# Sample states, convolution rows and vectors in the chip's order, and the samples' state step on turned states

## The chip, the cores and the metric

The kernel runs on one core of a Trainium2 chip. It is one launch. The metric is the device time of that launch in microseconds (us). The engines named below are those of the profile: PE is TensorE's matrix multiply and PEld its weight load, DVE is VectorE, ACT is ScalarE, POOL is GpSimd, and SP is SyncE, whose queue issues nearly all transfers (DMAs) of this kernel. Each engine takes its instructions strictly in the order in which they were written into its stream, and an instruction that waits for a semaphore holds up all that stand behind it.

## The reference, cut to what matters

One step of a decoder with two layers: first a Mamba-2 state-space layer (SSD), then latent attention (MLA). A prompt of 1024 tokens and 8 samples of 8 tokens each go through both. Only the SSD layer, and in it mostly the samples' part, is touched here.

```python
def causal_conv(xbc, buf, w, b):              # xbc: 4096 columns; buf: the last 3 rows of each sample
    full = jnp.concatenate([buf, xbc], axis=1)
    out = full[:, 0:t] * w[0]
    for k in range(1, 4):
        out = out + full[:, k:k + t] * w[k]
    return out + b, full[:, full.shape[1] - 3:]          # the second result is returned: new state_conv

def ssd_scan(x, dt, a_head, bm, cm, init_state):         # 32 heads of 64, 8 groups of 4 heads, state width 128
    ...
    def step(s, inp):                                    # s: (heads, 64, 128) for each sample or the prompt
        st, dec = inp
        return dec[..., None, None] * s + st, s
    final, prev = lax.scan(step, init_state, (states, chunk_decay))
    y_off = jnp.einsum('bclgn,bcgrpn->bclgrp', cc, prev) * decay_in[..., None]
    y = (y_diag + y_off).reshape(b, L, h, p)
    return y, final                                      # final is returned: new state_ssm
```

For a sample the scan has one step: the new state of each head is a decay times the old state (64 by 128, `state_ssm`), plus an outer product summed over the 8 tokens of B (128 wide) with the weighted inputs x (64 wide). The samples' output `y` takes C (128 wide) times the old state.

## The kernel before, in words

All products run on PE in float32 halves: a value is split into a high part (a cast on ACT) and a low part (value minus high part, on DVE or POOL; `split`, lines 125 to 133), and three products replace one.

The SSD layer has 8 groups of 4 heads. A group has a projection part (`Group`): four blocks of 128 columns (B, C and two of x), each made in three pieces of 24 matmuls into the PSUM tile `pj` (line 86; two such tiles take turns), copied to `raw` by ACT (lines 508 to 511), then convolved with 1 step on ACT (line 521) and 3 on DVE (line 525), then Silu on ACT (line 481). `gates` makes nine more pieces `pz` (line 98) that ACT copies to `z` and puts through Silu in three instructions (lines 569, 571, 572).

Then the group is scanned. `ssd_chunks` goes through the eight chunks of the prompt and the samples' tokens as a ninth: it reads a block `M` of cumulative decays by a DMA (line 627; three such tiles take turns), adds a mask on DVE (628), takes Exp on ACT in four instructions (632), multiplies on DVE (633), and multiplies with x on PE (`py`, 637). `ssd_states` does the samples' states in four parts per group (two halves of the samples, `q`, by two pairs of heads, `pr`): a state tile `s0` is loaded (711), turned on PE by four transposes into the PSUM tile `s0p` (714), split into `sh` and `sl`, multiplied with C (`pv`, 723); POOL multiplies the loaded tile with the decay (727), PE makes the outer product `sn` (730) from x and a copy `bb` of B that POOL spread over four samples (705), DVE adds it (732), and the tile is stored (733). The state tile lies with head and head-row on the partitions and the state width along them, as in the reference; the product with C needs it the other way round.

The projection of group g+1 and the scan of group g are written in turns (`layer_ssd`), and a scheduler that plans with its own table of times then sets the order in which the instructions stand in each engine's stream. So a change to a few instructions can move others. The tables that Exp and Silu need on ACT are not the same, and an `ACT_TABLE_LOAD` stands wherever the two follow each other.

Vectors (norm weights, convolution weights) are loaded as rows and turned on PE (lines 199 to 209); the samples' convolution rows are loaded as 96 rows and turned by eight transposes (`conv_state_T`, 356 to 362); the new rows of a group, collected in `ct` by POOL (518, 519), are turned by four transposes into `ctp` (533), copied to `co` by DVE (535), which takes a `raw` tile for it, and stored by six DMAs (538, 539). The prompt's last state is turned by two transposes (`pf`, 666), copied (668) and stored (669).

## Time and profile before

| what | us |
|---|---|
| median of 3 runs (1922.32 to 1925.89) | 1924.01 |
| the profiled execution's own time | 1926.24 |
| its span | 1924.4 |
| PE busy | 1890.9 (98%) |
| DVE busy | 1206.0 (63%) |
| ACT busy | 1102.0 (57%) |
| POOL busy | 823.3 (43%) |

The profile is of one execution, 2.23 us above the median. The span is the time from its first to its last instruction, and 1.84 us lie around it. PE's busy time counts matmuls that overlap, so that it does not say how fast PE works; what one matmul costs is read from the chain that ended last, which counts it from its start to the next one's. The SSD layer takes about the first half of the span: norm and the first group's projection until about 119 us, eight scans until about 890 us, and the output product until about 1010 us. The rest is MLA.

### The profile page before, as it was taken

The page shows a single profiled execution, that of the slowest core. Times are in us where ns is not written, and L with a number is a line of the kernel's source. Part 1 is how long each engine was busy: PE and PEld are TensorE (multiplying, and loading weights), DVE is VectorE, ACT ScalarE, POOL GpSimd, SP SyncE. Part 2 cuts the span into 40 slices and gives each one's busy share as a digit, 9 for nine tenths or more (in the row PEclk, how much of TensorE's full clock was granted, in tenths as well). Part 3 has the DMA queues.
Part 4 walks back from the last instruction along what each step waited for, and adds up shares of the span by engine and source line. Part 5 has one row for each costly group of instructions (what it writes and reads, how often), then busy time and mean ns, then how long its engine had stood idle before and what let it go on. Part 6 is the DMA issues. An engine that isn't in the chain of part 4 may idle for free.

```text
span 1924.4 us, 33639 instructions
## 1 busy us (share of the span) xinstructions
PE 1890.9 (98%) x12023; PEld 1728.8 (90%) x12023; DVE 1206.0 (63%) x2500; ACT 1102.0 (57%) x2523; POOL 823.3 (43%) x1122
## 2 busy tenths in 40 slices
PE   8999999999999999999999999999999999899998
PEld 7999999999999999888788998998888888788887
DVE  5557676757676757665534114567877888766674
ACT  6467566667666666733214314436777777755552
POOL 2447555545654555443004222104433435774551
PEclk9999999999999999999999999999999999999999
DMA  5223323333333232645534343123111112754541
GB/s 165 53 78 91 96 79 98 86 104 86 97 83 98 85 98 81 212 152 175 164 109 129 114 163 87 63 102 96 49 47 41 52 41 60 207 185 150 156 129 39
DMA packets 181087, 202.02 MB, mean 105 GB/s; under 512 B 18828, under 2 KB 147608, under 8 KB 180536
## 3 DMA queue, kind: packets, MB, share of 16 engines
q1 hardware_dynamic: 175864, 180.08, 30.9%
q0 software_dynamic: 4976, 19.66, 3.2%
q8 instruction: 95, 1.56, 0.4%
q14 instruction: 72, 0.59, 0.1%
q10 hardware_dynamic: 80, 0.13, 0.0%
HBM read 146.52 MB, written 53.28 MB: 104 GB/s over the span
## 4 chain that ended last, share of the span: by engine, by line
PE 84%; ACT 4%; DVE 4%; DMA 4%; issue 2%; POOL 1%; SPq 0%; POOLq 0%; DVEq 0%; ACTq 0%
PE pj L86 22%; PE pz L98 7%; PE pq L98 6%; PE pob L98 5%; PE p L98 5%; PE poa L98 3%; PE py L637 2%; PE sc L86 2%; PE o L86 2%; PE sc L1376 2%; PE o L1439 2%; PE o L1441 2%; PE st L1408 2%; PE st L1409 2%; PE st L1410 2%
## 5 line engine op out<-in xcount | busy, mean ns | idle before, releaser
L86 PE MATMUL pj<-xl,wih 128*128 128x384 f32 (+1 forms) x768 | 255.4, 333 | 0.0
L86 PE MATMUL pj<-xh,wih 128*128 128x384 f32 (+1 forms) x768 | 252.9, 333 | 1.2 <-ACT xh L273 0.9
L86 PE MATMUL pj<-xh,wil 128*128 128x384 f32 (+1 forms) x768 | 252.9, 329 | 0.0
L1422 POOL TENSOR_TENSOR tl<-P,th 128x384 fp32r<-128x384 f32 (+1 forms) x96 | 90.5, 942 | 234.3 <-ACT P L1420 192.7
L525 DVE SCALAR_TENSOR_TENSOR acc<-raw,vec,acc 128x1112 f32<-128x1112 f32 x96 | 140.9, 1469 | 14.9 <-ACT acc L521 14.0
L86 PEld LDWEIGHTS pj<-xh,wih 128*128 128x128 f32 x768 | 143.8, 188 | 2.6 <-ACT xh L273 1.4
L86 PEld LDWEIGHTS pj<-xl,wih 128*128 128x128 f32 x768 | 144.5, 188 | 1.0
L86 PEld LDWEIGHTS pj<-xh,wil 128*128 128x128 f32 x768 | 144.5, 188 | 0.5
L98 PE MATMUL pz<-wih,xh 128*128 128x256 f32 x504 | 143.2, 288 | 1.2 <-ACT z L566 1.2
L98 PE MATMUL pz<-wil,xh 128*128 128x256 f32 (+1 forms) x504 | 139.7, 283 | 0.0
L1419 ACT ACTIVATE th<-st 128x512 fp32r<-128x512 f32 x192 | 94.8, 494 | 66.7 <-PE st L1415 51.0
L98 PE MATMUL pz<-wih,xl 128*128 128x256 f32 x448 | 128.5, 287 | 0.0
L632 ACT ACTIVATE M<-M,tok 128x128 f32<-128x128 f32 (+1 forms) x288 | 90.8, 388 | 58.5 <-DVE M L628 58.1
L1712 POOL TENSOR_TENSOR kvl<-pgr,kvh 128x256 fp32r<-128x256 f32 x128 | 97.3, 787 | 57.0 <-ACT kvh L1710 52.6
L133 DVE TENSOR_TENSOR wil<-wraw,wih 128x512 fp32r<-128x512 f32 x88 | 73.9, 845 | 39.6 <-ACT wih L127 33.6
L98 PEld LDWEIGHTS pz<-wih,xh 128*128 128x128 f32 x504 | 95.9, 190 | 2.2 <-ACT z L566 1.7
L1420 ACT ACTIVATE P<-st 128x512 f32<-128x512 f32 x192 | 93.8, 489 | 0.0
L98 PEld LDWEIGHTS pz<-wil,xh 128*128 128x128 f32 (+1 forms) x504 | 92.8, 184 | 0.1
L1422 DVE TENSOR_TENSOR tl<-P,th 128x512 fp32r<-128x512 f32 x96 | 74.3, 774 | 19.6 <-ACT P L1420 19.5
L98 PEld LDWEIGHTS pz<-wih,xl 128*128 128x128 f32 x448 | 85.3, 190 | 0.7
L613 POOL TENSOR_TENSOR xdd<-xsT,tok 128x256 f32<-128x256 f32 x64 | 48.7, 761 | 86.8 <-ACT xsT L599 83.9
L127 ACT CAST wih<-wraw 128x512 fp32r<-128x512 f32 x92 | 56.1, 618 | 44.9 <-PE pj L86 29.4
(833 smaller groups left out, 6274.6 us busy)
## 6 DMA issues: line engine op xcount, KB each, us to landing
wraw<-in_ssd_w_in SPq DMA_DIRECT2D x92, 256.0 KB
M<-acs_d SPq DMA_DIRECT2D x64, 256.0 KB
s<-in_state_ssm SPq DMA_DIRECT2D x32, 256.0 KB
y_d<-y SPq DMA_DIRECT2D x64, 128.0 KB
out_s_ssm<-s SPq DMA_DIRECT2D x32, 256.0 KB
q_d<-qt SPq DMA_DIRECT2D x32, 192.0 KB
qp<-q_d SPq DMA_DIRECT2D x8, 768.0 KB
wraw<-in_ssd_w_out SPq DMA_DIRECT2D x10, 512.0 KB
```

Of the source, the lines that this page charges most:

```text
L86: nc.tensor.matmul(out, a, b, start=(i == 0), stop=(i == n - 1))
L98: nc.tensor.matmul(o, a, b, start=(j == 0), stop=(j == len(ops) - 1))
L127: k.cast = nc.scalar.copy(hi, src)
L133: return (eng or nc.vector).tensor_tensor(lo, src, hi.bitcast(F32), op=ALU.subtract)
L525: last = nc.vector.scalar_tensor_tensor(acc, raw[:, j : j + n], k.convw[j][:, blk : blk + 1], acc, op0=ALU.mult, op1=ALU.add)
L613: nc.gpsimd.tensor_tensor(v3(xdd), v3(xsT), hb(2), op=ALU.mult)
L632: nc.scalar.activation(M[:m, h, :m], M[:m, h, :m], AF.Exp, bias=tk[:, 0, 4 * g + h : 4 * g + h + 1])
L637: nc.tensor.matmul(py[:m, h * 64 : h * 64 + 64], M[:m, h, :m], xsT[:m, h * 64 : h * 64 + 64], start=True, stop=True)
L1419: nc.scalar.activation(th[:, :n], ps[:, :n], AF.Exp, scale=SCALE)
L1420: nc.scalar.activation(P[:, :n], ps[:, :n], AF.Exp, scale=SCALE)
L1422: eng.tensor_tensor(tl[:, :n], P[:, :n], th[:, :n].bitcast(F32), op=ALU.subtract)
L1712: nc.gpsimd.tensor_tensor(rl[:, j], raw[:, j], rh[:, j].bitcast(F32), op=ALU.subtract)
```

## The change

numpy lays out four inputs before the launch and puts three outputs into the reference's order after it. In the kernel:

- The vectors come as one tile of 128 by 196 by one DMA; the five loads, two transposes and a copy go.
- The samples' convolution rows come in the order of `convT` by one DMA; four loads, eight transposes and two copies go.
- The new convolution rows are stored as they lie in `ct`, by one DMA per group; four transposes, a copy and five DMAs per group go.
- The prompt's last state is stored as it lies; two transposes and a copy per group go.
- The samples' states come with the state width on the partitions. The four transposes per part go, and `split` reads the loaded tile in SBUF. The decay is multiplied along the other axis (its small table `decs` is made by one matmul with ones and has 256 columns instead of 128), and the outer product is made the other way round: B is now the operand that is loaded, and x is spread over the samples by POOL, once for each pair of heads (`xb`, two per half instead of one `bb`).

```diff
-def load_vectors(k, vp, psum):
+def load_vectors(k):
     nc, I, cp = k.nc, k.I, k.cp
     nc.sync.dma_start(k.ident, I["c_ident"])
-        r1 = vp.tile([128, 128], F32, name="r1")
-        nc.sync.dma_start(r1, I["ssd_conv_w"].rearrange("o k (b c) -> (o k b) c", c=128))
...
-        nc.tensor.transpose(p[:, :128], r1, k.ident)
-        nc.tensor.transpose(p[:, 128:196], r2, k.ident[:68, :68])
-        nc.vector.tensor_copy(k.vec, p[:, :196])
+    k.vec = cp.tile([128, 196], F32, name="vec")
+    nc.sync.dma_start(k.vec, I["vec"])
...
             def after():
-                conv_state_T(k, p0, psum)
+                k.nc.sync.dma_start(k.convT, k.I["state_conv"])
...
     def conv_out(self):
-        for bi in range(4):
-            nc.tensor.transpose(p[:27, bi * 128 : bi * 128 + 128], self.ct[:, bi], k.ident)
-        co = self.rp.tile([128, RAW], F32, tag="raw", name=f"co{g}", bufs=2)[:27, :512]
-        nc.vector.tensor_copy(co, p[:27])
-        sc = k.O["s_conv"].rearrange("o b w c -> (o b w) c")
-        for o, n, c in ((0, 128, DIN + 128 * g), (128, 128, DIN + 1024 + 128 * g), (256, 256, 256 * g)):
-            nc.sync.dma_start(k.O["p_conv"][0, 0, :, c : c + n], co[0:3, o : o + n])
-            nc.sync.dma_start(sc[:, c : c + n], co[3:27, o : o + n])
+        k, g = self.k, self.g
+        k.nc.sync.dma_start(k.O["conv"][g], self.ct)
...
         if i == 7:
-            for pr in range(2):
-                nc.tensor.transpose(pf[:, pr * 128 : pr * 128 + 128], S[:, pr * 128 : pr * 128 + 128], k.ident)
-            fo = sp.tile([128, 256], F32, tag="fo", name="fo" + tag, bufs=1).rearrange("p (a n) -> p a n", a=2)
-            nc.scalar.copy(fo, pf[:, :256].rearrange("p (a n) -> p a n", a=2))
-            nc.sync.dma_start(k.O["p_ssm"][0, 0, 4 * g : 4 * g + 4].rearrange("(a h) p n -> (h p) a n", h=2), fo)
+            nc.sync.dma_start(k.O["p_ssm"][g], S)
...
-        bb = sp.tile([96, 4, 128], F32R, tag="bb", name=f"bb{tag}{q}", bufs=1)
-        nc.gpsimd.tensor_tensor(bb, b3.bitcast(F32).unsqueeze(1).to_broadcast([96, 4, 128]),
-                                k.blk3.unsqueeze(2).to_broadcast([96, 4, 128]), op=ALU.mult)
         for pr in range(2):
             s0 = sp.tile([128, 4, 128], F32, tag="s0", name=f"s0{tag}{q}{pr}", bufs=2)
-            nc.sync.dma_start(s0, I["state_ssm"][0, bs, h0 : h0 + 2].rearrange("b h p n -> (h p) b n"))
-            for b in range(4):
-                nc.tensor.transpose(pt[:, b * 128 : b * 128 + 128], s0[:, b], k.ident)
+            nc.sync.dma_start(s0, I["state_ssm"][pair][:, bs])
+            xb = sp.tile([96, 4, 128], F32R, tag="bb", name=f"xb{tag}{q}{pr}", bufs=1)
+            nc.gpsimd.tensor_tensor(xb, x3[:, 128 * pr : 128 * pr + 128].bitcast(F32).unsqueeze(1).to_broadcast([96, 4, 128]),
+                                    k.blk3.unsqueeze(2).to_broadcast([96, 4, 128]), op=ALU.mult)
...
-            split(k, sh, sl_, pt)
+            split(k, sh, sl_, s0.rearrange("p b n -> p (b n)"))
...
-            nc.gpsimd.tensor_tensor(s0, s0, k.decs[:, h0 // 2, bs].unsqueeze(2).to_broadcast([128, 4, 128]),
+            nc.gpsimd.tensor_tensor(sv, sv, k.decs[:, bs, h0 : h0 + 2].unsqueeze(3).to_broadcast([128, 4, 2, 64]),
                                     op=ALU.mult)
-            nc.tensor.matmul(pt, x3[:, pr * 128 : pr * 128 + 128], bb.rearrange("p b n -> p (b n)"),
-                             start=True, stop=True)
+            nc.tensor.matmul(pt, b3, xb.rearrange("p b n -> p (b n)"), start=True, stop=True)
...
-            nc.sync.dma_start(k.O["s_ssm"][0, bs, h0 : h0 + 2].rearrange("b h p n -> (h p) b n"), s0)
+            nc.sync.dma_start(k.O["s_ssm"][pair][:, bs], s0)
```

The scheduler writes another order. Line numbers of the changed kernel are smaller, by 11 at the norm and by 39 to 46 in the scan. First PE, at the first samples' part of the scan of group 2. Before, the four transposes stand in the first chunk's products:

```order
L86 MATMUL st_0_3798<-xddh_0_3777,BTh_0_3771 128x256
L86 MATMUL pj<-xh,wih 128x384
L714 MATMUL s0p_800_3875<-ident,s_800_3873 128x128 x4
L86 MATMUL st_0_3798<-xddl_0_3778,BTh_0_3771 128x256
L86 MATMUL st_0_3798<-xddh_0_3777,BTl_0_3772 128x256
L637 MATMUL py_0_3793<-xsT_0_3769,M_0_3785 128x64 x4
```

Now the product with C (`pv`, line 677) stands there, since it needs nothing of PE ahead of it:

```order
L598 MATMUL py_0_3684<-xsT_0_3660,M_0_3676 128x64 x4
L86 MATMUL st_0_3689<-xddh_0_3668,BTh_0_3662 128x256
L677 MATMUL pv_800_3770<-sh_800_3766,cblk_1091 64x128
L677 MATMUL pv_800_3770<-sl_800_3767,cblk_1091 32x128 x2
L677 MATMUL pv_800_3770<-sh_800_3766,cblk_1091 64x128
L86 MATMUL st_0_3689<-xddl_0_3669,BTh_0_3662 128x256
```

The transposes are gone, and `pv` has moved up to the place where they stood. Next ACT, where group 1's last gate piece meets the scan of group 2. Before, all Silus of `z` (line 572 is the last) stand ahead of the next Exp (632):

```order
L572 ACTIVATE z_3635<-z_3635 64x256
L127 CAST wih<-wraw 128x512
L632 ACT_TABLE_LOAD
L632 ACTIVATE M_1_3982<-M_1_3982,tok 128x128 x4
L661 ACTIVATE xD_8_3693,yssq<-y_8_3710 64x256
L127 CAST wih<-wraw 128x512
L508 COPY raw_3822<-pj 128x384
```

Now an Exp (593) stands ahead of the last Silu (533), and the tables change twice more:

```order
L593 ACT_TABLE_LOAD
L593 ACTIVATE M_1_3868<-M_1_3868,tok 128x128 x4
L127 CAST xddh_0_3668<-xdd_0_3666 128x256
L127 CAST wih<-wraw 128x512
L533 ACT_TABLE_LOAD
L533 ACTIVATE z_3526<-z_3526 64x256
L655 CAST x_80_3756<-xf_80_3754 96x256
L658 CAST b_80_3759<-x3p_80_3746 96x128
L127 CAST wih<-wraw 128x512
L477 COPY raw_3713<-pj 128x384
L593 ACT_TABLE_LOAD
L593 ACTIVATE M_2_3972<-M_2_3972,tok 128x128 x4
```

The stream has the same at the end of each of six groups: line 572 of before has 2 table loads ahead of its Silu and line 632 has 22 ahead of its Exp; now these are 8 and 28. Last SP at the start. Before, six loads of constants stand between the prompt's rows and the first weights:

```order
L751 DMA xt2_137<-in_x_prompt 128x1024
L196 DMA ident_58<-in_c_ident 128x128
L199 DMA r1_147<-in_ssd_conv_w 128x128
L201 DMA r2_149<-in_norm_w 16x128
L202 DMA r2_149<-in_ssd_conv_b 32x128
L203 DMA r2_149<-in_ssd_norm_w 16x128
L204 DMA r2_149<-in_mla_q_norm_w 4x128 [waits DMAHW0_49]
L318 DMA wraw_159<-in_ssd_w_in 128x4x128 [waits DMAHW1_49]
```

Now two do, and the first weights wait for no earlier transfer's semaphore (there are eight of these, DMAHW0 to DMAHW7, used in turn):

```order
L705 DMA xt2_137<-in_x_prompt 128x1024
L196 DMA ident_58<-in_c_ident 128x128
L198 DMA vec_147<-in_vec 128x196
L307 DMA wraw_149<-in_ssd_w_in 128x4x128
L307 DMA wraw_155<-in_ssd_w_in 128x4x128
L307 DMA wraw_161<-in_ssd_w_in 128x4x128
L307 DMA wraw_167<-in_ssd_w_in 128x4x128 [waits DMAHW0_49]
```

Four loads of weights have moved up by four places.

74 lines of the change are left out of this document (32 added, 42 removed).

## The prediction

> **What bounds the kernel now.** I read the page's busy times first, then the stretches by stage, then the chain that ended last, stage by stage, and last the rows of the instructions that go or come.
>
> ```profile
> span 1924.4 us, 33639 instructions
> PE 1890.9 (98%) x12023; PEld 1728.8 (90%) x12023; DVE 1206.0 (63%) x2500; ACT 1102.0 (57%) x2523; POOL 823.3 (43%) x1122
> 119.00:215.00 96.00, 95.01 (x705) 92.64 (x705) 69.38 (x117) 67.35 (x178) 64.01 (x88) 1.00 0.38 108
> ...
> 311.00:407.00 96.00, 95.64 (x710) 94.14 (x708) 64.50 (x106) 63.58 (x160) 51.33 (x82) 1.00 0.32 91
> ...
> 800.00:890.00 90.00, 88.25 (x505) 74.39 (x504) 59.86 (x121) 37.13 (x110) 38.87 (x58) 1.00 0.52 170
> ```
>
> The last three lines are the first, the third and the last of the eight scans: start and end, length, then the busy us of PE, PEld, DVE, ACT and POOL, the granted clock, the DMA share and GB/s. PE stands still for 0.4 to 1.8 us of a scan of some 96 us; each of the others has a quarter of it free or more. So PE's work is the first suspect, and the clock is 1.00 throughout. But a busy PE can still be ahead of something. The chain tells in what share of a scan PE itself carries the end. Here are its shares by line for the first, the sixth and the last scan:
>
> ```profile
> by line: PE pz L98 21.4%; issue 13.3%; PE pj L86 9.9%; DMA M<-acs_d 4.5%; DMA wraw<-in_ssd_w_in 4.1%; PE py L637 3.5%; POOL y L657 3.2%; POOL xdd L613 2.6%; POOL xddl L133 2.4%; POOL Sl L133 2.2%; DVE y L660 2.1%; DVE acc L525 2.0%; ACT wih
> ...
> by line: PE pj L86 49.3%; PE pz L98 26.5%; PE py L637 7.1%; PE st L86 3.2%; PE py L86 2.9%; PE pv L723 2.0%; PE cb L625 1.9%; PE s0p L714 1.8%; PE sn L730 1.1%; PE trp L594 1.1%; PE trp L595 1.0%; PE trp L597 0.9%; PE x3p L693 0.7%; PE ctp
> ...
> by line: PE poa L98 52.0%; DMA wraw<-in_ssd_w_out 7.3%; issue 7.1%; DMA M<-acs_d 3.9%; PE py L637 3.7%; PE ytpa L826 3.4%; DVE M L628 2.6%; PE st L86 2.4%; DVE xl L771 2.0%; PE py L86 1.8%; PE pv L723 1.8%; PE cb L625 1.5%; DVE yla L133 1.5
> ```
>
> What isn't PE's adds up to 36% in the first scan (issue, the DMAs of M and of weights, POOL, DVE), to nothing in the sixth and to 24% in the last. Between them the other five have 8 to 36%. The mean share of PE over the eight scans is so at most about 82%.
>
> **The transposes.** The chain gives what one costs PE's stream, from its start to the next instruction's:
>
> ```profile
> 33.67 0.33 PE cvp L361 x4
> ...
> 57.36 0.22 PE ctp L533 x2
> ...
> 298.90 0.22 PE pf L666 x2
> ...
> 304.16 3.85 PE pj L86 x22
> ...
> 308.29 0.44 PE s0p L714 x4
> ```
>
> These are 0.11 us for each of ctp, pf and s0p and 0.08 us for cvp. (A single one's record is longer, but it overlaps the next.) The counts:
>
> ```profile
> L361 PE MATMUL cvp<-ident,cst x8: 243/244/248, 33.5 to 35.2; 96*128 96x96 f32 x8
> ...
> L533 PE MATMUL ctp<-ident,ct x32: 270/272/293, 57.2 to 760.2; 128*27 128x128 f32 x32
> ...
> L666 PE MATMUL pf<-ident,S x16: 270/271/272, 198.6 to 889.3; 128*128 128x128 f32 x16
> ...
> L714 PE MATMUL s0p<-ident,s x128: 270/272/276, 125.4 to 875.5; 128*128 128x128 f32 x128
> ```
>
> Ahead of the first scan 8 x 0.08 + 4 x 0.11 = 1.1 us go, in a stretch where the chain runs on PE: I take all of it. In the scans 128 + 28 + 16 = 172 transposes go, 172 x 0.11 = 18.9 us of PE. If PE carried everything, 18.9 us would be won; if each scan gave only the first one's share (64%), 12.1. I take the mean share, 0.82 x 18.9 = 15.5 us. The matmul `sn` keeps its size (96 rows, 512 columns) and `decs` its sum of columns (two matmuls of 128, now one of 256): nothing.
>
> **The start.** The first weights are issued late, because of SP's constants and their semaphores:
>
> ```profile
> 4.78 0.37 SPq L204 DMA_DIRECT2D r<-in_mla_q_norm_w  x1
> 5.98 2.86 SPq L318 DMA_DIRECT2D wraw<-in_ssd_w_in  x4
> ...
> 9.05 0.36 DVE L209 COPY vec<-vecp 128x196 f32<-128x196 f32 x1
> ...
> 10.38 0.75 DVE L258 TENSOR_SCALAR xt<-xt,rs 128x1024 f32<-128x1024 f32 x1
> ...
> 11.76 0.62 ACT L127 CAST wih<-wraw 128x512 fp32r<-128x512 f32 x1 [0.23 <-DMA wraw<-in_ssd_w_in]
> ...
> 12.29 1.05 ACT L273 ACTIVATE xh<-xtp,vec 128x384 fp32r<-128x384 f32 x2
> ...
> 12.92 0.62 PE L86 MATMUL pj<-xh,wih 128*128 128x384 f32 x2 [0.86 <-ACT xh L273]
> ```
>
> The third cast of weights, at 11.76, waits for its transfer, and the first `xh`, without which PE can't begin, stands behind it. In the new order the weights are issued about 2 us earlier, and the copy of 0.36 us no longer stands ahead of the scaling at 10.38. The `xh` still needs that scaling (end 11.13) and the transposes of it (0.4 us). So it can start at about 11.2 instead of 12.29. I take 1.2 us; the bounds are 0 (the data come no sooner, being already bound by the rate of all queues) and 1.5.
>
> **What is added, and what hides it.** On ACT, twelve more table loads:
>
> ```profile
> L632 ACT ACT_TABLE_LOAD x22 | 28.2, 1283 | 0.4
> L572 ACT ACT_TABLE_LOAD x2 | 2.6, 1283 | 0.0
> L668 ACT COPY fo<-pf 128x256 f32<-128x256 f32 x8 | 3.0, 371 | 7.7 <-PE pf L666 7.5
> ...
> 298.82 0.30 ACT L127 CAST Ch<-acc 128x128 fp32r<-128x128 f32 x1 [3.49 <-PE py L86]
> ...
> 308.20 0.62 ACT L127 CAST wih<-wraw 128x512 fp32r<-128x512 f32 x1 [2.84 <-DMA wraw<-in_ssd_w_in]
> ```
>
> That is 12 x 1.283 = 15.4 us of ACT, less 3.0 for the copies of `fo`: two loads, 2.6 us, at the end of each of six groups. Behind them stand the copies of `pj`, for which PE waits when both of its tiles are full. One tile is 24 matmuls of about 0.17 us (3.85 us for 22 in the chain above), so ACT may be 4 us late before PE feels it, and just there ACT has holes of 3.49 and 2.84 us. I take 0; bounds 0 and 15.4.
>
> On POOL, 32 copies `xb` take the place of 16 `bb`; on DVE, the 32 low parts `sl` now read two tiles in SBUF instead of one in PSUM:
>
> ```profile
> L705 POOL TENSOR_TENSOR bb<-b,blk x16: 1030/1037/1542, 128.9 to 847.7; 96x512 fp32r<-96x512 f32 x16
> ...
> L133 DVE TENSOR_TENSOR wil<-wraw,wih 128x512 fp32r<-128x512 f32 x88 | 73.9, 845 | 39.6 <-ACT wih L127 33.6 <-PE pj L86 3.1 <-issue 2.1
> L133 DVE TENSOR_TENSOR sl<-s0p,sh 128x512 fp32r<-128x512 f32 x32 | 21.8, 682 | 2.1 <-ACT sh L127 2.1
> ...
> L727 POOL TENSOR_TENSOR s<-s,decs 128x512 f32<-128x512 f32 x32 | 35.2, 1099 | 17.3 <-PE s0p L714 17.3
> ```
>
> POOL gets 16 x 1.04 = 16.6 us more, 2.1 in a scan of which it has 32 or more free. The nearest row to the new `sl` is `wil`, the same size with both sources in SBUF: 845 ns instead of 682, so 32 x 0.16 = 5.2 us more on DVE, against 8 copies `co` of 0.67 us that go. The decay on POOL waited for the transposes and now waits for `sl`, one cast and one subtraction later. In the first scan POOL is on the chain with 10.4% or more, so there its 2.1 us may show with 0.2 us. I take 0.5 us in all for these; bounds 0 and 16.6. On SP, 48 short transfers become 8, and the state tiles move in longer runs; no transfer of either stands in the chain's lists above, so nothing is taken for them.
>
> **Sum.** 1.1 + 15.5 + 1.2 - 0.5 = 17.3 us less. Against the profiled execution's own 1926.24 us that is 1908.9; against the median of the runs, which is 2.2 lower, 1906.7. MLA, from about 1010 us on, keeps its order of instructions on PE.
>
> **The rivals.**
>
> *All of it, and more.* The scheduler fills PE with other work when it can, so that a part of the chain that isn't PE's may just be slack that PE's work covers. For this speaks that PE is busy 95 of 96 us. Then 18.9 + 1.1 + 1.5 = 21.5 go, and with half of the 1 us that PE stands still in each of eight scans, 25.5: 1898 to 1903.
>
> *Part is given back.* The first scan's POOL, the one PSUM bank of `sn` (held from the matmul until DVE's addition, which now waits for the later decay), or contention of `sl` with POOL put waits of about 1 us into each scan: 17.3 - 8 = 9 us less, 1912 to 1920. Against it, PE waited little for the copy of B:
>
> ```profile
> PE sn L730 <- POOL bb L705: 0.6, 2, 0.4
> ```
>
> *Slower: the copies of `pj` come late.* In each of six groups' ends an Exp of M now stands on ACT ahead of the last Silu of z and of the next group's first copy of `pj`. That Exp waits for DVE, and DVE for the DMA of M:
>
> ```profile
> ACT M L632 <- DVE M L628: 58.1, 31, 3.7
> ```
>
> Its longest wait is 3.7 us. With two loads and the Silu (2.57 + 0.42) that makes 6.7 us in front of the copies. PE's cover is about 4 us. From 2.9 us of waiting at each of the six (17.3 / 6) the gain is gone. With the whole cover 6 x 2.7 = 16 us are lost, 1923; with none 6 x 6.7 = 40, 1947; the middle is 1935. So it is slower only where PE's second tile is full already when the Exp begins to wait. The new order was planned with M's DMA issued in time, and ACT's holes there speak against it.
>
> *No change.* The loads alone, all on PE's path, take 15.4 of 17.3 us: 1922.
>
> The Trainium skill (ScalarE: Activation LUTs, "What ACT_TABLE_LOAD costs") gives a load 1283 ns and adds a drain of about 1380 ns, 2.66 us for each switch. By that the twelve would cost 31.9 us, an estimate from that page, and with all of it on the path the kernel would take 1938 us. In this trace a load starts within 0.02 us of the end of the instruction ahead of it, and the next one starts 0.02 us after it:
>
> ```profile
> 289.93 0.27 ACT L127 CAST BTh<-trp 128x128 fp32r<-128x128 f32 x1
> 290.21 1.28 ACT L569 ACT_TABLE_LOAD   x1
> 291.51 1.27 ACT L569 ACTIVATE z<-z 128x1280 f32<-128x1280 f32 x1
> ```
>
> No drain is seen, so the sum keeps 1.283.
>
> **How the numbers follow.** About 0.2% (3.8 us) is what a measurement of this kernel can tell from no change. I give the forecast, 1903 to 1912, 0.45; all of it and more 0.18; part given back 0.20; the loads on the path, within 0.2%, 0.07; slower 0.10. So faster is 0.83, the same 0.07 and slower 0.10. The time is the first case's, 1907. The range has to leave out no more than 2 in 10: 1898 to 1921 takes in the first three cases and the edge of the fourth, and leaves out the slower one and a little below.
>
> **What would show it.** In the profile of the changed kernel PE's count in a scan is lower by about 22 with no more idle time, and the shares of the chain on PE are no smaller. PE's first `pj` starts at about 11.7 instead of 12.92. ACT has 8 and 28 loads at the two lines and no wait of PE for a copy of `raw`. `xb` and the decay are no long wait of PE or DVE. I am wrong if PE's idle time at the ends of groups grows by 3 us each, if the chain in the scans moves to POOL or ACT, or if the new order leaves PE short of work in a place that the rows of before can't show.

## The result, and the profile after

The changed kernel is slower. Its median is 1931.97 us (five runs, 1929.34 to 1936.31) against 1925.43 for the kernel before on the same chip (1922.32 to 1925.96). The ratio is 1.0038, with a 95% interval of 1.0020 to 1.0056: 7 us, where 17 less had been forecast. The profiled execution took 1931.98 us.

First the page of the changed kernel: its span, the busy times, and the shares of the chain that ended last.

```profile
span 1930.2 us, 33140 instructions
PE 1877.8 (97%) x11835; PEld 1714.4 (89%) x11835; DVE 1222.1 (63%) x2489; ACT 1112.8 (58%) x2527; POOL 867.6 (45%) x1135
...
PE 81%; ACT 6%; DVE 6%; POOL 3%; DMA 2%; issue 2%; SPq 0%; POOLq 0%; DVEq 0%; ACTq 0%
```

PE lost 188 instructions and 13.1 us of busy time (1890.9 before). The span grew by 5.8. So PE's idle time grew by 18.9 us: all that was taken from PE, and more, came back as waiting. The same three scans as in the prediction, in stretches of the changed kernel (start and end, length, busy us of PE, PEld, DVE, ACT, POOL, granted clock, DMA share, GB/s):

```profile
119.00:216.00 97.00, 93.58 (x694) 91.03 (x693) 71.40 (x117) 69.92 (x178) 65.23 (x90) 1.00 0.34 103
312.00:409.00 97.00, 94.68 (x684) 92.62 (x684) 65.25 (x102) 64.90 (x159) 57.31 (x83) 0.98 0.31 87
802.00:892.00 90.00, 87.53 (x495) 74.36 (x494) 62.98 (x125) 38.67 (x109) 42.08 (x61) 0.98 0.51 176
```

PE stood still for 0.4 to 1.8 us of a scan; now it is 2.3 to 3.4. And the clock, 1.00 throughout before, is 0.98 in two of the three. The chain's shares by line in the sixth scan of the changed kernel, where before all was PE's:

```profile
by line: PE pj L86 48.6%; PE pz L98 15.6%; PE py L598 5.7%; PE py L86 2.6%; POOL xdd L574 2.3%; PE st L86 2.3%; ACT M L593 2.1%; ACT acc L450 2.1%; issue 2.1%; PE pv L677 2.0%; PE cb L586 1.9%; POOL xD L584 1.7%; ACT L450 1.3%; ACT L593 1.3
```

POOL's xdd and xD, ACT's Exp of M, its Silu of acc and two table loads are on it now. The waits of PE and then of ACT in the six scans in the middle (190 to 785 us) of the changed kernel (us in total, times, longest):

```profile
PE pz L98 <- ACT z L527: 5.1, 5, 1.2
PE py L86 <- ACT Sh L127: 3.1, 4, 1.1
PE st L86 <- POOL xddl L133: 2.2, 5, 0.6
...
ACT xddh L127 <- POOL xdd L574: 30.3, 19, 4.6
```

Before, PE's two largest waits there, and ACT's for xdd, were these:

```profile
PE cb L625 <- DVE yo L726: 1.5, 4, 0.4
PE pz L98 <- ACT z L566: 0.9, 1, 0.9
...
ACT xddh L127 <- POOL xdd L613: 8.4, 13, 1.4
```

PE's wait for a copy of z comes five times in six scans. One of them, at 280 us, shows how it arises. These are rows of the timeline of the changed kernel, first POOL, then DVE, ACT and PE (start, duration, engine and line, operation, and in brackets the idle time ahead of it and who ended it):

```profile
269.13 1.04 POOL L667 TENSOR_TENSOR xb<-x,blk 96x512 fp32r<-96x512 f32 x1
...
270.27 0.61 POOL L574 TENSOR_TENSOR xdd<-xsT,tok 128x256 f32<-128x256 f32 x1
270.85 1.68 POOL L584 TENSOR_TENSOR xD<-xsT,dsk 128x256 f32<-128x256 f32 x1
272.49 0.72 POOL L133 TENSOR_TENSOR xddl<-xdd,xddh 128x256 fp32r<-128x256 f32 x1
273.17 1.69 POOL L584 TENSOR_TENSOR xD<-xsT,dsk 128x256 f32<-128x256 f32 x1
274.83 1.68 POOL L574 TENSOR_TENSOR xdd<-xsT,tok 128x256 f32<-128x256 f32 x1
...
270.22 1.83 DVE L494 SCALAR_TENSOR_TENSOR acc<-raw,vec,acc 128x1112 f32<-128x1112 f32 x1 [0.31 <-ACT acc L490]
...
272.18 2.21 DVE L494 SCALAR_TENSOR_TENSOR acc<-raw,vec,acc 128x1112 f32<-128x1112 f32 x1
...
274.65 1.39 DVE L494 SCALAR_TENSOR_TENSOR acc<-raw,vec,acc 128x1112 f32<-128x1112 f32 x1
...
276.54 0.41 ACT L127 CAST xddh<-xdd 128x256 fp32r<-128x256 f32 x1 [4.58 <-POOL xdd L574]
276.96 1.28 ACT L450 ACT_TABLE_LOAD   x1
278.26 2.06 ACT L450 ACTIVATE acc<-acc 128x2224 f32<-128x2224 f32 x1
280.22 0.35 ACT L527 COPY z<-pz 128x256 f32<-128x256 f32 x1
...
280.63 0.39 PE L98 MATMUL pz<-wih,xh 128*128 128x256 f32 x1 [1.04 <-ACT z L527]
```

POOL does the spread copy xb, a first xdd, two xD and only then the second xdd, at 274.83. Three of its instructions of 128 by 256 take 1.68 us there instead of 0.61, while three steps of the convolution run on DVE. ACT stands for 4.58 us at the cast of that second xdd. Behind the cast stand a table load, a Silu of 2.06 us and the copy of z for which PE waits. So here lateness on POOL went through ACT's strict order to PE, and hardly anything in these rows is about the transposes. It is one path of the loss; the experiments below do not show it to be the main one.

The other steps that the prediction named: the first weights did come earlier, but PE's first pj started at 12.28 (12.92 before, 11.7 expected). MLA begins with the load of a table on ACT (line 963 here, line 1009 before). It stands at 1029.2 us in this profile and at 1025.4 in that of before. So in this pair of profiles the SSD layer, the only part that was changed, is 3.8 us longer. From there to the end it is 901.0 us, 899.1 before; over all the profiles of this study that stretch lies between 895 and 903, so nothing is to be read from that difference.

### The profile page after: what moved, and what is told of

Same layout as the page of the kernel before. It is cut to its first block, busy times and chain, and to the rows that moved or that the text cites. A ratio compares the mean times of both kernels' runs of the same rounds, so it can differ in the third digit from the quotient of the medians.

```text
span 1930.2 us, 33140 instructions
## 1 busy us (share of the span) xinstructions
PE 1877.8 (97%) x11835; PEld 1714.4 (89%) x11835; DVE 1222.1 (63%) x2489; ACT 1112.8 (58%) x2527; POOL 867.6 (45%) x1135
## 4 chain that ended last, share of the span: by engine, by line
PE 81%; ACT 6%; DVE 6%; POOL 3%; DMA 2%; issue 2%; SPq 0%; POOLq 0%; DVEq 0%; ACTq 0%
PE pj L86 21%; PE pq L98 6%; PE pz L98 6%; PE p L98 5%; PE pob L98 5%; PE poa L98 4%; PE sc L86 2%; PE o L86 2%; PE sc L1330 2%; PE o L1393 2%; PE py L598 2%; PE o L1395 2%; PE st L1362 2%; PE st L1363 2%; PE st L1364 2%
## 5 line engine op out<-in xcount | busy, mean ns | idle before, releaser
L494 DVE SCALAR_TENSOR_TENSOR acc<-raw,vec,acc 128x1112 f32<-128x1112 f32 x96 | 157.4, 1640 | 13.6 <-ACT acc L490 12.5
L589 DVE TENSOR_TENSOR M<-M,negu 128x512 f32<-128x512 f32 x64 | 57.6, 901 | 28.8 <-DMA M<-acs_d 28.5
L584 POOL TENSOR_TENSOR xD<-xsT,dsk 128x256 f32<-128x256 f32 (+1 forms) x72 | 68.5, 952 | 12.0 <-ACT xsT L560 7.7
```

The source lines that it names most:

```text
L494: last = nc.vector.scalar_tensor_tensor(acc, raw[:, j : j + n], k.convw[j][:, blk : blk + 1], acc, op0=ALU.mult, op1=ALU.add)
L584: nc.gpsimd.tensor_tensor(v3(xD), v3(xsT), k.dsk[:m, hs].unsqueeze(2).to_broadcast([m, 4, 64]), op=ALU.mult)
L589: nc.vector.tensor_tensor(M[:m, :, :m], M[:m, :, :m], (k.negs if smp else k.negu)[:m, :m].unsqueeze(1).to_broadcast([m, 4, m]), op=ALU.add)
```

## The experiments

All ratios are to the kernel before, run on the same chip beside the experiment (its median was 1923.3 to 1925.4 in every set), with 95% intervals. "PE idle" is from 116 to 900 us, "POOL busy" from 0 to 1030, and "MLA begins" is the start of MLA's first table load, all in us and all of the one profiled execution; the last tells how long the SSD layer took there. Two of these executions are not typical: that of `before_bb32` was the fastest of its six (1930.6, 7 us below the median), that of `no_decay` the slowest of its eleven (1929.7, 6 above).

| run | median us | ratio | PE idle | POOL busy | MLA begins |
|---|---|---|---|---|---|
| before | 1925.4 | 1 | 7.4 | 471 | 1025.4 |
| changed kernel | 1932.0 | 1.0038 [1.0020, 1.0056] | 22.2 | 514 | 1029.2 |
| layouts alone | 1926.6 | 1.0009 [0.9996, 1.0022] | 14.1 | 484 | 1025.2 |
| state step alone | 1921.5 | 0.9987 [0.9975, 0.9998] | 13.7 | 513 | 1020.6 |
| Exps held back | 1928.5 | 1.0019 [1.0006, 1.0033] | 23.5 | 511 | 1028.9 |
| layouts alone, Exps held back | 1925.6 | 1.0013 [0.9999, 1.0027] | 11.4 | 484 | 1024.7 |
| B spread once a half | 1924.6 | 1.0004 [0.9990, 1.0018] | 16.8 | 488 | 1022.0 |
| both of these | 1922.2 | 1.0000 [0.9988, 1.0011] | 14.9 | 490 | 1019.0 |
| no spread copies after the first | 1912.5 | 0.9947 [0.9932, 0.9962] | 14.6 | 499 | 1012.5 |
| no decay on POOL | 1923.9 | 1.0001 [0.9991, 1.0011] | 21.5 | 480 | 1025.3 |
| before, with 32 spread copies | 1937.9 | 1.0082 [1.0062, 1.0101] | 14.0 | 497 | 1033.5 |
| state step alone, B spread once a half | 1936.3 | 1.0057 [1.0038, 1.0076] | 19.7 | 480 | 1033.7 |
| 128 transposes put back | 1931.4 | 1.0037 [1.0021, 1.0053] | 14.3 | 505 | 1029.9 |
| before, with 128 more transposes | 1947.7 | 1.0119 [1.0096, 1.0142] | 11.7 | 462 | 1045.3 |
| xD behind xddl | 1920.4 | 0.9977 [0.9962, 0.9991] | 17.6 | 505 | 1018.9 |
| before, xD behind xddl | 1926.4 | 1.0014 [1.0000, 1.0028] | 7.0 | 501 | 1026.3 |
| both, B spread by ACT | 1918.5 | 0.9975 [0.9961, 0.9989] | 13.4 | 474 | 1015.2 |
| the same, xD behind xddl | 1913.7 | 0.9934 [0.9913, 0.9956] | 10.3 | 491 | 1014.5 |
| xD behind, 128 transposes put back | 1922.6 | 0.9988 [0.9978, 0.9997] | 9.9 | 526 | 1021.1 |
| the fastest, 128 transposes put back | 1930.5 | 1.0031 [1.0020, 1.0043] | 8.1 | 488 | 1026.7 |

**Each part alone.** `layout_only` is the changed kernel with `ssd_states` and the table `decs` of before; `states_only` is the kernel before with these two of the changed kernel.

```diff
-            nc.sync.dma_start(s0, I["state_ssm"][pair][:, bs])
+            nc.sync.dma_start(s0, I["state_ssm"][0, bs, h0 : h0 + 2].rearrange("b h p n -> (h p) b n"))
...
-            split(k, sh, sl_, s0.rearrange("p b n -> p (b n)"))
+            split(k, sh, sl_, pt)
```

> The changed kernel with the samples' state step as it was before (states as in the reference, transposes on PE, one spread copy of B); the vectors, convolution rows and the prompt's last state stay as changed. POOL theory (POOL's 16 more copies, and the SBUF port that it shares with DVE, make POOL late in the scans, and PE waits for what comes behind it): this part adds nothing to POOL, so it is faster by its own 58 transposes and its start, 5 to 7 us, 1918 to 1920. ACT theory (twelve more table loads at the ends of six groups make ACT late): the stream has as many loads as before, so 1918 to 1920 as well. Order theory (a new order from the scheduler is worse or better by itself, whatever the work): anything from 1915 to 1933.

> The kernel before with only the samples' state step of the changed kernel (turned states, B loaded, x spread by POOL for each pair of heads, decay table of 256 columns). Its stream has 50 table loads, two fewer than before and fourteen fewer than the changed kernel. POOL theory: the whole loss is here, 1932 to 1940. ACT theory: without the loads the 128 transposes are won, 1910 to 1915. Order theory: anything from 1910 to 1933.

The POOL and the ACT theory failed in both, with all four of their ranges; the ranges of the order theory, 1915 to 1933 and 1910 to 1933, hold both results, but they leave out next to nothing. The layouts, which take 58 transposes away and were to win 6 us, won nothing (1.0009). The state step, which has all the new copies on POOL, was not the culprit by itself (0.9987). The two effects add up to a ratio of 0.9996, and together they give 1.0038. What the parts cost depends on what else stands in the streams.

**The table loads.** In groups 1 to 6 the second chunk's Exps are held behind the last Silu of z. In the changed kernel (`exp_behind`) this saves two loads a group, 52 in all instead of 64. `layout_exp` is the same edit of the layouts alone.

```diff
+            if 0 < g < G - 1 and i == 1:
+                es.enter_context(k.tc.issue_after(gr.zlast.ins))
             for h in range(4):
                 nc.scalar.activation(M[:m, h, :m], M[:m, h, :m], AF.Exp, bias=tk[:, 0, 4 * g + h : 4 * g + h + 1])
```

> The changed kernel, where the Exps of each scan's second chunk are issued behind the last Silu of the gates in groups 1 to 6, so that the stream has the 52 table loads of before instead of 64. ACT theory: the forecast comes true, 1907 to 1914. POOL theory: POOL's work is as in the changed kernel, so at most 3 us better than it, 1928 to 1933.

> The changed kernel with the samples' state step of before (so the layouts alone), and with the second chunk's Exps held behind the last Silu of z in groups 1 to 6. If the twelve table loads are what took back the gain of the 58 transposes that the layouts remove, 1926.6 - 5 = 1920 to 1922; if they cost here what they cost the changed kernel, 3.5 us: 1923; if the layouts' copies on POOL are what took it back: 1925 to 1927.

The changed kernel won 3.5 us by medians, as the POOL theory had it; MLA begins 0.3 us earlier, and the intervals overlap. So the twelve loads, 15.4 us of ACT, cost about a quarter of that or less. They are not the main cause. `layout_exp` says nothing of their price, against what its expectation takes for granted: the layouts alone have the 52 loads of before already, and ACT has 2515 instructions in `layout_only` and in `layout_exp`. Its 1925.6 lies in the range given for copies on POOL, but the layouts add none (1122 instructions on POOL, as before). All that it shows is that holding these Exps back changes nothing where no load is saved (1.0013 against 1.0009).

**POOL's spread copies, more and fewer.** `spread_b` spreads B once for each half, as before the change, and makes the product in four pieces; `both` adds the Exps of above.

```diff
-            xb = sp.tile([96, 4, 128], F32R, tag="bb", name=f"xb{tag}{q}{pr}", bufs=1)
-            nc.gpsimd.tensor_tensor(xb, x3[:, 128 * pr : 128 * pr + 128].bitcast(F32).unsqueeze(1).to_broadcast([96, 4, 128]),
-                                    k.blk3.unsqueeze(2).to_broadcast([96, 4, 128]), op=ALU.mult)
...
-            nc.tensor.matmul(pt, b3, xb.rearrange("p b n -> p (b n)"), start=True, stop=True)
+            for b in range(4):
+                nc.tensor.matmul(pt[:, 128 * b : 128 * b + 128], bb[:, b], x3[:, 128 * pr : 128 * pr + 128],
+                                 start=True, stop=True)
```

> The changed kernel with B spread over the samples once per half, as before (16 copies on POOL instead of 32), each sample's copy loaded for a matmul with 128 columns of x (four matmuls of 128 columns in place of one of 512; the granted work on PE is the same within 1 us). It still has 64 table loads. POOL theory: POOL loses 16 to 18 us of work and what that did to DVE, so 1910 to 1920. ACT theory: no better than the changed kernel, 1929 to 1933.

> The changed kernel with both edits: B spread once per half (16 copies on POOL), and the Exps of a scan's second chunk behind the last Silu of the gates (52 table loads). If what the two edits won by themselves adds up (7.4 us and 3.5 us against the changed kernel's 1932), 1921. If one and the same wait was shortened by both, no better than the better one, 1924 to 1926. If PE is what is left as the bound, the forecast's 1907.

The first won 7.4 us, less than was expected of it, and the two together 9.7, where the sum would be 10.9. By the ratios it is 6.5 and 7.3 us, where the sum would be 10.2, and the interval of `both` overlaps that of `spread_b`; so it is not shown that the two add up. The next two runs take more off POOL, and leave out what their expectations name. `xb_once` makes the spread copy in the first scan only; `no_decay` drops the multiplication of line 682.

> The changed kernel, but the spread copy of x is made on POOL once, in the first scan, and used for all 32 outer products (the new sample states are then not the reference's). POOL has 31 instructions and about 35 us less than in the changed kernel. POOL theory: twice what the 17 us of the kernel with B spread once per half won, so 1915 to 1918. Order theory (the order of the streams decides, not how much POOL has to do): no better than 1924.

> The changed kernel without the multiplication of the sample states by their decay on POOL (the new sample states are then not the reference's): 32 instructions and 40 us of POOL less. POOL theory: 1913 to 1918, as for the spread copy made once. If it is the place of the spread copy in the chain (x, its low part, spread copy, outer product, addition) rather than POOL's load: no better than 1926.

And `before_bb32` adds nothing to the kernel before but the second spread copy of each half; `states_bb` is the state step alone with the edit of `spread_b`.

```diff
-        bb = sp.tile([96, 4, 128], F32R, tag="bb", name=f"bb{tag}{q}", bufs=1)
+            bb = sp.tile([96, 4, 128], F32R, tag="bb", name=f"bb{tag}{q}{pr}", bufs=1)
```

> The kernel before, in which only the spread copy of B is made twice per half, once for each pair of heads, as the changed kernel does with x: POOL gets 16 instructions and about 17 to 19 us more, nothing else changes. POOL theory: as much slower as the changed kernel got faster when it lost them, 7 us: 1929 to 1933. Order theory: within 3 us of before, 1921 to 1927.

> The kernel before with the samples' state step on turned states, and with the samples' B spread once for each half of them (the four products of 128 columns of the run that did this to the changed kernel), so that POOL has the spread copies of before, 16, and PE has lost the 128 transposes. If the 7.4 us that this edit gave the changed kernel come again, 1921.5 - 7.4 = 1914. If the step's other moves (the split from SBUF rather than from PSUM on DVE, the decay's four-way shape) have eaten the transposes' worth by themselves: 1919 to 1923. A pure PE theory (128 x 0.11 x 0.8 = 11 us less than before) gives 1913.

Sixteen more POOL instructions of about 1.2 us cost the kernel before 14 us (1.0082), with PE busy 98% of the time. Not making 31 of the 32 in the changed kernel won 19. Both are more than the POOL theory gave, and the SSD layer shows both: MLA begins 8.1 us later in the first, 16.7 earlier in the second. So these copies are dear. These two runs also leave the order of the streams near to what it was: up to 1030 us, counted from the traces by operation and tiles, 676 of POOL's 724 instructions in `before_bb32` and 682 of 710 in `xb_once` keep their order. But the sum of POOL's work is not the measure: `xb_once` has only 14 us less of it; without the decay POOL has 34 us less, and the kernel is only 8 us faster (MLA begins 3.9 us earlier), which meets neither range of `no_decay`. PE's idle time is there the same as without that edit (21.5 against 22.2), though of its slowest execution. Nor is the path shown at 280 us the measure. In `xb_once` PE still waits five times for z, and ACT waits for xdd nearly as long:

```profile
PE pz L98 <- ACT z L527: 3.4, 5, 0.7
...
ACT xddh L127 <- POOL xdd L574: 27.4, 14, 4.2
```

Which waits gave the 19 us was not followed. The decay is needed only for the last addition to a state and its store; the spread copy stands between x3 and the product, and ahead of the chunks' work. `states_bb` is the plain miss: the edit that won 7.4 us in the changed kernel lost 15 in the state step alone, though POOL had 33 us less there. Part is PE's: busy time rose from 1880.6 to 1888.1. Four products of 128 columns take more than one of 512: the records of sn add up to 18.8 us instead of 13.5 (18.9 instead of 13.7 in `spread_b`, whose expectation had PE's work the same within 1 us). Most of the rest is 6.0 us more of idle time, and its cause stays open.

**Transposes, put back and added.** `pe_back` lets PE make the 128 transposes of the state parts again, with no reader; `pe_twice` makes them twice in the kernel before.

```diff
+            pd = psum.tile([128, 512], F32, tag="tr", name=f"s0p{tag}{pr}{q}", bufs=PB["tr"])
+            for b in range(4):
+                nc.tensor.transpose(pd[:, b * 128 : b * 128 + 128], s0[:, b], k.ident)
             split(k, sh, sl_, s0.rearrange("p b n -> p (b n)"))
```

> The changed kernel with the 128 transposes of the state parts put back on PE: 16 in each of the eight scans, of the same loaded rows into the same pair of banks of PSUM as before the change, with nothing reading what they write, so that PE has its old load and all else is as changed. PE theory (what a transpose costs PE, 0.11 us, stands on the path by PE's share of the chain, some 0.8): 128 x 0.11 x 0.8 = 11 us more than the changed kernel, 1941 to 1946. POOL theory (in the scans after the change PE waits for what POOL and ACT hand it, so that taking transposes away had bought idle time): the same work put back fills that idle time, and costs 0 to 5 us: 1930 to 1936.

> The kernel before with each of the 128 transposes of the state parts made twice, into the same place: 128 more on PE, nothing else. If PE's work was on the path in the scans before the change, as the prediction had it: 128 x 0.11 x 0.82 = 11.5 us more, 1934 to 1937. If the scans were set there too by what is handed to PE: 0 to 4 us more, 1924 to 1928.

No other pair of the study differs as much. The changed kernel takes the same time with these transposes as without (1.0037 and 1.0038). In the kernel before 128 more cost 1.19%, 23 us, which is above both ranges. PE's line on the page, of `pe_back` and then of `pe_twice`:

```profile
PE 1889.3 (98%) x11963; PEld 1728.1 (90%) x11963; DVE 1215.0 (63%) x2489; ACT 1112.9 (58%) x2527; POOL 859.8 (45%) x1135
```

```profile
PE 1909.8 (98%) x12151; PEld 1746.0 (90%) x12151; DVE 1195.7 (61%) x2500; ACT 1095.5 (56%) x2521; POOL 818.8 (42%) x1122
```

In `pe_back` PE is busy 11.5 us longer and idle 11.8 us less than in the changed kernel. In `pe_twice` it is busy 18.9 us longer than before, and idle time rises too. The transposes themselves are 14.8 us of that, 0.12 each, by the rows of s0p up to 1035 us, of before and of `pe_twice`; 1.7 us more is a stretch at half the clock (524 to 532 us).

```profile
L714 PE MATMUL s0p<-ident,s 128*128 128x128 f32 x128 | 20.5, 272 | 0.0
...
L714 PE MATMUL s0p<-ident,s 128*128 128x128 f32 x256 | 35.3, 272 | 0.0
```

So in the kernel before, added work of PE lengthens the time by its price and more, as the prediction would have it; in the changed kernel the same work shows nowhere. But neither run changes PE's work alone, since the scheduler writes a new order for each: 607 of POOL's 722 instructions up to 1030 us in `pe_back` keep the order of the changed kernel, and 644 of 707 in `pe_twice` that of the kernel before, where the added transposes also stand ahead of the split that reads the tile. In `pe_back` the five waits for z are gone, though nothing was done about them. PE's two largest waits in the six scans are now

```profile
PE st L86 <- POOL xddl L133: 3.9, 7, 0.6
PE py L86 <- ACT Sh L127: 2.1, 6, 0.4
```

So the transposes may be free there because PE had idle time for them, or because a better order paid for them; the runs can't tell the two apart.

**The order on POOL.** `xd_behind` holds the product xD behind the low part of xdd in all groups, which the kernel does in the first and the last only. No instruction is added or taken away. `before_xd` is the same edit in the kernel before.

```diff
-        with k.tc.issue_after(behind.ins) if not smp and g in (0, G - 1) else nullcontext():
+        with k.tc.issue_after(behind.ins) if not smp else nullcontext():
             nc.gpsimd.tensor_tensor(v3(xD), v3(xsT), k.dsk[:m, hs].unsqueeze(2).to_broadcast([m, 4, 64]), op=ALU.mult)
```

> The changed kernel with POOL's product xD held behind the low part of xdd in all groups (it was so in the first and last only); no work is added or taken away. The scheduler then sets xdd and xddl of the second chunk ahead of both spread copies xb on POOL's stream. Order theory (ACT stands up to 4.6 us at the cast of xdd, 30 us in six scans, and PE's copies are behind it): that wait falls below 15 us, PE's five waits of 1.04 us for z go, and 5 to 10 us are won: 1922 to 1927. Load theory (POOL's total counts, wherever it stands): no change, 1930 to 1933.

> The kernel before with the same edit (xD held behind the low part of xdd in all groups). There ACT's waits for xdd are not among the six largest, so the order theory expects within 3 us of before: 1921 to 1927. If the edit is good or bad by itself, whatever the spread copies: the same step as in the changed kernel.

This edit won 11.6 us by medians (1.0038 to 0.9977, intervals apart), more than the 5 to 10 of the order theory and more than any work taken off POOL except the spread copies as a whole. More than xD moved with it: 602 of POOL's 736 instructions up to 1030 us keep the order of the changed kernel. In the kernel before it won nothing (1.0014). The same place of the second scan, POOL's and then ACT's rows of `xd_behind`:

```profile
267.14 0.61 POOL L574 TENSOR_TENSOR xdd<-xsT,tok 128x256 f32<-128x256 f32 x1
267.71 1.04 POOL L667 TENSOR_TENSOR xb<-x,blk 96x512 fp32r<-96x512 f32 x1
268.71 0.73 POOL L133 TENSOR_TENSOR xddl<-xdd,xddh 128x256 fp32r<-128x256 f32 x1
269.40 0.61 POOL L584 TENSOR_TENSOR xD<-xsT,dsk 128x256 f32<-128x256 f32 x1
...
268.06 0.41 ACT L127 CAST xddh<-xdd 128x256 fp32r<-128x256 f32 x1
268.36 0.39 ACT L527 COPY z<-pz 128x256 f32<-128x256 f32 x1
```

xdd is ready before this xb (the other one stood ahead of both, at 262.74), the cast on ACT waits for nothing and z is copied at once. In the six scans ACT's wait for xdd and PE's for its hand-overs are now:

```profile
PE py L86 <- ACT Sh L127: 3.7, 5, 1.1
PE pv L677 <- DVE M L594: 3.4, 4, 1.1
...
ACT xddh L127 <- POOL xdd L574: 16.8, 10, 4.0
```

The five waits for z are gone; ACT's wait is 16.8 us, where below 15 was expected. That order on POOL counts, and not only its load, is what this run shows. It does not show that ACT's wait for xdd is the way: the fastest version below has 30.5 us of that wait, and 3.3 us of PE's for z.

**A version that beats both.** `bb_act` is `both` with B spread by ACT (four scaled copies of 96 by 128) instead of POOL; `bb_act_xd` also holds xD behind.

```diff
-        nc.gpsimd.tensor_tensor(bb, b3.bitcast(F32).unsqueeze(1).to_broadcast([96, 4, 128]),
-                                k.blk3.unsqueeze(2).to_broadcast([96, 4, 128]), op=ALU.mult)
+        for b in range(4):
+            nc.scalar.activation(bb[:, b], b3.bitcast(F32), AF.Copy, scale=k.blk3[:, b : b + 1])
```

> The changed kernel with B spread once for each half, the Exps held back, and the spread copy made by ACT (four scaled copies of 96x128) in place of POOL's one: POOL has 16 x 1.04 = 17 us less than in the run with both edits. POOL theory: each us of POOL taken from the step's chain gave about one us there: 1922.2 - 8 to 17 = 1905 to 1914. If ACT's four copies lengthen the same chain as much (four of some 0.25 us in the place of one of 1.04): 1920 to 1924. If ACT is the tighter of the two in the scan: above 1924.

> The changed kernel with B spread once for each half by ACT, the second chunk's Exps held back, and xD held behind the low part of xdd in all groups. Without the last it took 1918.5, with ACT waiting 19 us in six scans for xdd and PE 5.4 for its low part. Order theory: 3 to 6 us less, 1912 to 1916. Load theory: 1918 again.

The first missed its expectation (1918.5, where 1905 to 1914 was given for POOL's load and 1920 to 1924 for a chain as long as before), the second met it. At 0.9934 [0.9913, 0.9956] it is faster than the kernel before by about 0.7%, and than the changed one by about 1%. Its page and the three scans:

```profile
PE 1874.0 (98%) x11931; PEld 1717.5 (90%) x11931; DVE 1192.4 (62%) x2489; ACT 1111.9 (58%) x2579; POOL 833.0 (44%) x1103
```

```profile
119.00:216.00 97.00, 94.66 (x716) 93.17 (x715) 70.70 (x121) 73.04 (x194) 59.91 (x86) 1.00 0.35 105
312.00:409.00 97.00, 94.71 (x703) 93.36 (x703) 62.88 (x103) 64.76 (x164) 53.10 (x79) 1.00 0.31 91
802.00:892.00 90.00, 89.54 (x511) 75.99 (x511) 53.65 (x116) 36.90 (x109) 36.02 (x56) 1.00 0.45 151
```

The clock is 1.00 in all three. Do the transposes count again? The 128 were put back into it and into `xd_behind`.

> The best version so far (B spread once for each half by ACT, Exps held back, xD behind; 1913.7) with the 128 transposes put back on PE. No spread copy stands on POOL, so the order there is as without them. If PE's work is on the path again: 11.5 to 14 us more, 1925 to 1928. If what is handed to PE still sets the pace: 1914 to 1918.

> The run that held xD behind the low part of xdd (1920.4), with the 128 transposes of the state parts put back on PE. The scheduler's order on POOL then has both spread copies xb ahead of the second chunk's xdd again, and only xD behind it. If the transposes count once ACT is fed in time: 128 x 0.11 x 0.82 to 1 = 11.5 to 14 us more, 1932 to 1934. If they are still free: 1920 to 1923.

In the fastest version they cost 0.97%, 19 us (17 by medians), above the 11.5 to 14 that was given; MLA begins 12.2 us later. So PE's work counts again there. In `xd_behind` they cost about 2 us (MLA begins 2.2 later), against my first expectation. There PE still had 17.6 us of idle time that took them in (9.9 with them); the fastest version had 10.3 (8.1 with them). So over the four kernels the 128 transposes cost 0 where PE idled 22 us, 2 where it idled 18, 19 where it idled 10, and 23 where it idled 7. That fits the reading that idle time takes them in; with a new order of the streams in each of the runs it does not prove it. `pe_back_xd` also speaks against that wait on ACT as the cause: both xb stand ahead of the second chunk's xdd again, ACT waits 35.5 us for xdd in six scans, more than in the changed kernel, and the time is 9 us less. What it shares with `xd_behind` is xD behind xddl.

## Why the prediction was wrong

*What bounds the kernel now: PE.* `pe_twice` bears it out for the kernel before, where it was even too low. I took 0.82 of a transpose's 0.11 us, by PE's mean share of the chain. The rows of s0p there show 14.8 us of PE for 128 more, and the time grew by 23, that is, by the whole price and more. What is beyond the price can be the new order's; that is open.

*The transposes, 15.5 us won.* Wrong. PE's busy time did fall by 13.1 us, or 18 with what the lower clock took. But nothing of it was left in the time, and `pe_back` shows that the changed kernel with 128 of the transposes on PE is as fast as without them. What failed is the step from "PE carries the chain" to "what leaves PE leaves the time". I took PE's being busy as proof that no other limit lay close behind it. One did: how soon POOL, DVE and ACT hand PE its work. PE's idle time in the scans went from 7.4 to 22.2 us. Their busy times, a quarter or more of them free, do not show it.

*What is added, and what hides it: POOL 0.5 us of 0 to 16.6.* This is the step that failed most. I compared 2.1 us with 32 us free in a scan. `before_bb32` puts a price on it in the kernel before: 14 us for the sixteen spread copies alone. That is within the bound of 16.6, but my value stood at the wrong end. A likely reason, which the rows suggest and no run isolates, is that the copy stands in a chain (x3, xb, sn) and ahead of xdd on an engine that works in order. I also put the order on POOL at nothing: `xd_behind`, which holds one instruction of each chunk back and takes no work away, won 11.6 us. The two prices may overlap, so they don't add up to the loss. In the state step alone (1921.5) the 14 us of the copies and the 14.8 us of PE that 128 transposes make would about cancel; that is a reading of the numbers, not a test.

*The table loads: 0, bounds 0 and 15.4.* The counts came as predicted (28 and 8 at the two lines), and `exp_behind` gives them 0.3 to 3.5 us. The small value was nearly right.

*DVE's sl, 5.2 us, hidden.* The row of `wil` gave nearly the right duration: 839 ns measured, 845 expected. That is partly luck, since in the other runs that read both tiles in SBUF it was 714 to 959. The lengthening went further than sl, to the convolution's steps and to POOL, as the section on the hardware shows; I had counted none of that.

*The start, 1.2 us.* 0.64 was seen at PE's first pj. The sign is right and the size unsettled: in the profiles with the new start pj begins between 11.5 and 13.0 us, in those with the old one between 12.3 and 13.1.

*The rivals.* "Part is given back" named contention of POOL and sl with waits of about 1 us a scan; the waits were of that size, but there were fourteen in the first three rows of PE's waits alone, for six scans. "Slower" had the shape of the path at 280 us, copies from PSUM late behind ACT's order, but named another copy (pj) and another cause (the Exp of M): PE's wait for raw was 1.0 us in all, its waits for z 5.1. Its chance of 0.10 was too small. The durations read from rows were nearly right (1.04 us for a spread copy, 1.14 measured); what the new order would put behind what had not been followed, although the prediction named it as the thing that could make it wrong.

What stays open: by which waits the spread copies and the order on POOL reach PE, why the layouts, which only take work away, win nothing by themselves, and why `states_bb` is slow. In every run the scheduler writes a new order for all engines, and none holds that order fixed.

## What to carry to other kernels

An engine that is busy 98% of the time may be bound by its work or by how exactly the others feed it; add the same work once more and see, since one kernel here paid 23 us for 128 transposes and the next one nothing, and compare the order of the streams before you read the result. When work is moved onto an engine that has time to spare, follow what will stand behind it in that engine's order, and what stands behind the instruction that waits for it on the next engine; the share of time that is free says nothing about that. Where a scheduler writes a new order for every edit, judge each part both alone and beside the others, and try to move work before taking it away.

## What the runs showed of the hardware

**POOL and DVE lengthen each other.** Groups of instructions up to 1035 us in the changed kernel (busy us and mean ns of one, then idle time ahead), and the same of the kernel before up to 1030:

```profile
L584 POOL TENSOR_TENSOR xD<-xsT,dsk 128x256 f32<-128x256 f32 x64 | 62.1, 971 | 0.0
...
L494 DVE SCALAR_TENSOR_TENSOR acc<-raw,vec,acc 128x1112 f32<-128x1112 f32 x96 | 157.4, 1640 | 13.6 <-ACT acc L490 12.5
L133 DVE TENSOR_TENSOR sl<-s,sh 128x512 fp32r<-128x512 f32 x32 | 26.8, 839 | 1.7 <-ACT sh L127 1.3
```

```profile
L623 POOL TENSOR_TENSOR xD<-xsT,dsk 128x256 f32<-128x256 f32 x64 | 49.4, 772 | 0.0
...
L525 DVE SCALAR_TENSOR_TENSOR acc<-raw,vec,acc 128x1112 f32<-128x1112 f32 x96 | 140.9, 1469 | 14.9 <-ACT acc L521 14.0
```

Neither instruction was changed, and xD is 26% longer, the convolution's step 12%. That is not a loss by itself: in `before_xd`, where nothing but an order was changed, xD took 924 ns, and the time rose by 0.14% only. In the timeline above the two engines take turns: the step at 270.22 ends at 272.05 and the xD begun at 270.85 ends 0.48 us later; the xD of 273.17 ends 0.47 after the step that ends at 274.39, and the xdd of 274.83 ends 0.47 after the step that ends at 276.04. Each of these three POOL instructions finishes half a microsecond after a DVE instruction does. The Trainium skill (SBUF — State Buffer, "Who interferes with whom") says that only the port pair which DVE shares with GpSimd makes the two contend, as an exclusive lock, and that a DVE instruction with two inputs in SBUF contends with a GpSimd instruction that reads SBUF, while one with at most one such input, outside the two-port modes, does not. The trace agrees, and by that page `sl` joined the contending ones with this change, since its input moved from PSUM to SBUF. The runs agree too: the mean of `sl` was 682 to 687 ns in the six kernels where one input is in PSUM, and 714 to 959 in the fourteen where both are in SBUF.

**The clock can drop after a short wait.** Three stretches of 4 us of the changed kernel (columns as in the stretches above):

```profile
376.00:380.00 4.00, 2.79 (x24) 2.51 (x22) 2.16 (x5) 3.95 (x5) 2.54 (x6) 1.00 0.08 26
380.00:384.00 4.00, 3.81 (x19) 3.51 (x20) 0.14 (x1) 3.99 (x13) 1.31 (x3) 0.57 0.37 73
384.00:388.00 4.00, 4.00 (x39) 3.96 (x38) 2.61 (x5) 3.40 (x12) 4.00 (x7) 1.00 0.11 42
```

PE stood still for 1.21 us ahead of 380, waiting for z, and then had 0.57 of the clock for one stretch: 1.72 us lost. In the scans of the changed kernel the losses are 1.7 and 1.7 (over two stretches) and once more 1.7, 5.2 us in all, and none in the scans of the kernel before or of the fastest version. So a wait of 1 us can cost 2.7. It need not: after the wait of 1.04 us for z at 280 the clock stayed at 1.00, and so it did after one of 1.34 us at 379 in the fastest version. The Trainium skill (TensorE: Matmul & The Clock Gate, Part 1) has half the clock for at least one window of about 3.4 us, from which a loss of 1.7 for one window is an estimate; the trace agrees with that size. It names an idle window of the same length as the cause, and here PE was busy for 2.79 of the 4 us.
